# Four hundred places later in the scheduler's priorities for one stream of a two-stream kernel

## The chip, the cores and the metric

The kernel runs on one core of a Trainium2 chip. The core has a matrix engine (TensorE, PE in the profile, with a separate row PEld for its weight loads), a vector engine (VectorE, DVE), a scalar engine for activations (ScalarE, ACT), a general engine (GpSimd, POOL, hardly used here) and a queue that issues transfers (SyncE, SP). Each works through its own list of instructions in order; they wait for one another by semaphores. The metric is the device time of one execution in microseconds (us). Before the change the median of three runs is 2886.37 us (2886.14 to 2888.42).

## The reference

The reference runs two networks one after the other on 256 tokens of width 1024, in float32. The first block has four layers; each is a mixer, a gated projection and a layer norm:

```python
for i in range(DEPTH):                       # mixers: conv, ssm, rwkv7, conv
    y = mixer[i % 3](x, ...)
    r = DN_ALPHA * x + y
    r = r + (p[i] @ ple_proj[i]) * jax.nn.sigmoid(r @ ple_gate[i])
    x = layer_norm(r, ln_g[i], ln_b[i])
```

The second block has two layers over the tokens x and over a context ctx of another 256 rows of the same width. Each layer is a half feed-forward, a mixer in which the tokens also look at the context, and another half feed-forward:

```python
x   = half_ffn(x,   ..., ffn_w1[l, 0], ffn_w3[l, 0], ffn_w2[l, 0])
ctx = half_ffn(ctx, ..., ffn_w1[l, 0], ffn_w3[l, 0], ffn_w2[l, 0])
# half_ffn: h + 0.5 * gate * (silu(m @ w1) * (m @ w3)) @ w2, m = modulate(rms_norm(h))
```

The context does not depend on the first block. Its first feed-forward can therefore be computed while the first block's tokens are still on their way.

## The kernel before

Activations lie transposed: 8 chunks of 128 features by 256 tokens. A weight tile is 128 x 1024 floats: it is loaded into `w` (4 buffers), ACT rounds it to fp32r (`whi`, L601), DVE forms the rest (`wlo`, L602), with 4 buffers for each of the two. Activations are split in the same way into a hi and a lo part. A product of one output tile (128 features x 256 tokens) is 24 matmuls: for each of 8 chunks the three products hi x whi, lo x whi and hi x wlo (`mm3` and `mm3g`, L433 in the profile, where the engine's helper issues them). They accumulate in one of three PSUM buffers `ps_mm`. Smaller products use `ps_st`, `ps_ca` and `ps_cb`.

The program is written as generators. The stream X is the first block: `first()` runs conv, ssm, rwkv and conv, each followed by `ple_norm`. The stream C is the context: in the first block only `ffn(0, 0, ctx, 1)` runs of it, and as much of the next work as its `wait` allows. It has 44 tiles of the inner product (names `h1_hi`, `h1_lo`, `td`) and 24 of the outer (names `d1_hi`, `d1_lo`), 1584 matmuls. `Net.weave` takes turns: it steps the first stream that its own clock model holds for ready, X before C. The order in which steps are taken is the order of the program. A scheduler then sets the order on every engine: it takes what is ready by its own estimates, and among that what stands first in the priorities. An instruction's priority is its place in the program, kept in `tc.cur_priority`.

Names that the change and the text use: in `ple_norm` the sums `total` and `r` go to PE, then the squares `sq`, then `tc` (the reciprocal root on ACT and DVE), then `r` and `x` per chunk. In `rwkv` the shift `dx` and the blend `ta` follow on DVE, with `mix_hi` on ACT and `mix_lo` on DVE. The heads are small products in `ps_cb` and `ps_st` with copies `rw_a`, `rw_b` and `sv` between them. `gs` and `g` are the gated outputs of rwkv and conv before their output product. `xs` is a layer norm's result, split for the next product. The profile leaves out the numbers of names, so the context's `h1_hi` and `d1_hi` read `h_hi` and `d_hi` there.

Of the kernel before, what the change touches and what calls it, by code (L numbers as in the profile page):

```python
# [72 lines left out]
class Cols:  # L73
    def __init__(self):
        self.at, self.parts, self.n = {}, [], 0
# [190 lines left out]
class Stream:  # L266
# [2 lines left out]

    def __init__(self, net, gen, cache=None, shared=()):  # L270
        self.net, self.gen, self.cache, self.shared = net, gen, cache, shared
        self.ready, self.done, self.req = 0.0, False, None
        self.other, self.alone = None, set()
        self.advance(None)

# [164 lines left out]
class Net:  # L440
# [95 lines left out]
    def weave(self, streams, until=None):  # L536

        while not (until() if until else all(s.done for s in streams)):
            while self.side is not None and not self.hold and self.next <= self.now() and (self.V.t < self.now() + SLACK or self.next < self.now() - LATE):
                gap = next(self.side, None)  # L540
                if gap is None:
                    self.side = None
                else:
                    self.next = max(self.next, self.now() - LATE) + gap
            live = [s for s in streams if not s.done and not s.blocked()]
            s = next((s for s in live if s.ready <= self.now()), None)
            if s is None:
                s = next((s for s in streams if not s.done and s.blocked() and s.ready <= self.now()), None)
            if s is None:
                self.idle += min(s.ready for s in streams if not s.done) - self.now() + 1e-6  # L550
            else:
                s.step()

    def par(self, gens, width, last=None, most=3):


        todo, live = iter(gens), []
        last = [last, 0.0, None] if last else None
        while True:
            while len(live) < width and (not live or self.chains < most):  # L560
                g = next(todo, None)
                if g is None:
                    break
                live.append([g, 0.0, None])
                self.chains += 1
            both = live + ([last] if last else [])
            if not both:
                return
            c = next((c for c in both if c[1] <= self.now()), None)
            if c is None:  # L570
                yield Until(max(min(c[1] for c in both), self.now() + 0.01))
                continue
            self.end = self.now()
            try:
                y = c[0].send(c[2])
            except StopIteration:
                if c is last:
                    last = None
                else:
                    live.remove(c)  # L580
                    self.chains -= 1
                continue
            c[2] = None
            if isinstance(y, tuple):
                c[2] = yield y
            else:
                c[1] = y if isinstance(y, Until) else self.end
# [1319 lines left out]
def program(tc, ap, out, pat, cat):  # L1907
    nc = tc.nc
    with ExitStack() as es:
        n = Net(tc, ap, pat, cat, es)  # L1910
        X = Stream(n, n.first())
        X.step()
        nc.sync.dma_start(out=n.pr, in_=ap["params"])

        g = pat["gains"]
        nc.vector.tensor_scalar(out=n.pr[:, g:], in0=n.pr[:, g:], scalar1=-0.5, scalar2=None, op0=ALU.mult)
        nc.vector.tensor_scalar(out=n.p("b_kvn", 0, 2), in0=n.p("b_kvn", 0, 2), scalar1=4.0, scalar2=None, op0=ALU.mult)
        n.consts("base")
        c = n.big("cond0")

        def load_context():
            nc.sync.dma_start(out=n.ctx, in_=ap["ctxT"])
            yield 1.0

        n.side = itertools.chain(n.ssm_prep(), load_context(), n.ada(c, [(0, i, (1,), GAPS[0] / 2) for i in range(PARTS)]))
        n.weave([X], lambda: n.parts[0][1] > 1 and n.stage != "")

        def tokens():
            yield from n.ffn(0, 0, x, 0)
            yield from n.mixer_ab(ab, 0, x, 0)  # L1930
            yield from n.ffn(0, 1, x, 0)
            yield from n.ffn(1, 0, x, 0)
            yield from n.mixer_cd(1, x)
            yield from n.ffn(1, 1, x, 0, True)

        def context():
            yield from n.ffn(0, 0, n.ctx, 1)
            yield from n.wait("tokens")
            yield from n.mixer_ab(ab, 0, n.ctx, 1)
            order.reverse()  # L1940
            yield from n.ffn(0, 1, n.ctx, 1)
            yield from n.ffn(1, 0, n.ctx, 1)
            yield from n.cd_ctx(1)

        cache, shared = {}, ("cd_f", "cd_v", "cd_k") + tuple(f"ffn_{p}10" for p in ("in", "out0", "out1", "out2"))
        C = Stream(n, context(), cache, shared)
        n.weave([X, C], lambda: X.done)
        x = n.out_x
        n.consts("second", n.big("second"))
        ab = n.ab_shared()  # L1950
        n.came.add("tokens")
        X = Stream(n, tokens(), cache, shared)
        C.other, X.other = X, C
        order = [C, X]
        n.weave(order)
        nc.sync.dma_start(out=out, in_=x)
# [16 lines left out]
```

## Time and profile before

| | before |
|---|---|
| median of 3 runs | 2886.37 us |
| profiled execution | 2890.76 us |
| its span | 2889.0 us |
| granted clock, mean | 0.977 |
| DVE busy | 2134.0 us (74%) |
| ACT busy | 1606.4 us (56%) |

The profile is of one execution, and its times are measured against that execution's 2890.76 us, of which 2889.0 us are the span from the first instruction to the last. Busy is the union of an engine's instructions. Matmuls are pipelined: each lasts longer than the step from its start to the next one's. So steps are read from starts, and waits from the brackets at a row's end, which give the idle time ahead of a row and the engine and tile that ended it.

### The profile page before, as it was taken

The numbers are of one execution on the slowest core, as the hardware profiler recorded it, in microseconds if no ns is written. First come the engines' busy times: TensorE is split into PE (matmuls) and PEld (weight loads), VectorE is DVE, ScalarE is ACT, GpSimd is POOL, SyncE is SP. The second block draws the span as 40 slices with busy tenths as digits, with TensorE's granted clock in tenths as the row PEclk, the third lists the DMA queues.
The fourth block names the chain that finished last, engine by engine and source line by source line (L and its number), as shares of the span: only waits on it lengthen the run. The fifth ranks groups of instructions, "written<-read, shape, count | busy, mean of one in ns | idle before, by whom it ended". The sixth has DMA issues, their size and how long they took to land.

```text
span 2889.0 us, 58552 instructions
## 1 busy us (share of the span) xinstructions
PE 2749.4 (95%) x23798; PEld 2604.6 (90%) x23798; DVE 2134.0 (74%) x3953; ACT 1606.4 (56%) x2976; POOL 14.8 (1%) x41
## 2 busy tenths in 40 slices
PE   8978799899999998999999999999999999999999
PEld 8967799778998998998999978999999999996999
DVE  8877777666688788899789887777855556676655
ACT  5455555766555465877666766445422234466443
POOL 0000000000000000000000000000000000000000
PEclk9989799999999999999999999999999999999999
DMA  7743355201586665666576644666543433222554
GB/s 270 238 165 110 108 167 175 82 17 40 163 269 226 220 197 167 209 215 203 182 226 195 199 130 155 203 225 194 180 142 125 139 117 103 89 82 65 161 182 139
DMA packets 132751, 467.53 MB, mean 162 GB/s; under 512 B 14720, under 2 KB 19072, under 8 KB 131840
## 3 DMA queue, kind: packets, MB, share of 16 engines
q1 hardware_dynamic: 132480, 463.78, 50.0%
q8 instruction: 187, 3.06, 0.4%
q14 instruction: 84, 0.69, 0.1%
HBM read 462.67 MB, written 1.05 MB: 161 GB/s over the span
## 4 chain that ended last, share of the span: by engine, by line
PE 72%; DVE 12%; DMA 7%; ACT 6%; issue 3%; SPq 0%; ACTq 0%; DVEq 0%
PE ps_mm L433 62%; PE ps_ca L433 5%; DMA w<-in_ada_dram 5%; DVE wlo L602 3%; PE ps_cb L433 2%; DVE junk L1379 2%; PE ps_st L433 2%; DVE ssm_m L403 2%; ACT whi L601 2%; DVE tc L403 1%; PE ps_cb L437 1%; ACT rw_b L403 1%; ACT L403 1%; ACT tc L403 1%; DMA w<-in_ab_in_dram 1%
## 5 line engine op out<-in xcount | busy, mean ns | idle before, releaser
L601 ACT ACTIVATE whi<-w 128x1024 fp32r<-128x1024 f32 (+1 forms) x687 | 715.9, 1043 | 740.2 <-PE ps_mm L433 488.1
L602 DVE TENSOR_TENSOR wlo<-w,whi 128x1024 fp32r<-128x1024 f32 (+1 forms) x687 | 825.6, 1203 | 239.2 <-ACT whi L601 236.8
L433 PE MATMUL ps_mm<-h_hi,whi 128*128 128x256 f32 x3024 | 873.1, 290 | 17.1 <-ACT h_hi L403 12.4
L433 PE MATMUL ps_mm<-h_hi,wlo 128*128 128x256 f32 x3024 | 859.5, 285 | 9.5 <-DVE wlo L602 9.5
L433 PE MATMUL ps_mm<-h_lo,whi 128*128 128x256 f32 x3024 | 856.5, 284 | 0.6 <-DVE h_lo L403 0.5
L433 PEld LDWEIGHTS ps_mm<-h_hi,whi 128*128 128x128 f32 x3024 | 573.6, 190 | 25.8 <-ACT h_hi L403 15.1
L433 PEld LDWEIGHTS ps_mm<-h_hi,wlo 128*128 128x128 f32 x3024 | 573.3, 190 | 12.2 <-DVE wlo L602 11.5
L433 PEld LDWEIGHTS ps_mm<-h_lo,whi 128*128 128x128 f32 x3024 | 577.5, 191 | 5.2 <-DVE h_lo L403 1.9
L1379 DVE SCALAR_TENSOR_TENSOR junk<-w,cond 128x1024 bf16<-128x1024 f32 x288 | 351.7, 1221 | 145.0 <-DMA w<-in_ada_dram 144.1
L433 PE MATMUL ps_mm<-d_hi,whi 128*128 128x256 f32 x1232 | 355.7, 289 | 4.1 <-DVE ctx L403 3.0
L433 PE MATMUL ps_mm<-d_hi,wlo 128*128 128x256 f32 x1232 | 350.4, 285 | 1.5 <-DVE wlo L602 1.5
L433 PE MATMUL ps_mm<-d_lo,whi 128*128 128x256 f32 x1232 | 349.2, 283 | 0.4 <-DVE d_lo L403 0.4
L433 PEld LDWEIGHTS ps_mm<-d_hi,whi 128*128 128x128 f32 x1232 | 232.3, 189 | 8.7 <-issue 5.7
L433 PEld LDWEIGHTS ps_mm<-d_lo,whi 128*128 128x128 f32 x1232 | 234.0, 190 | 3.4 <-issue 1.2
L433 PEld LDWEIGHTS ps_mm<-d_hi,wlo 128*128 128x128 f32 x1232 | 232.1, 189 | 2.8 <-DVE wlo L602 2.0
L403 DVE TENSOR_TENSOR td<-td,ps_mm 128x256 f32<-128x256 f32 x154 | 64.4, 418 | 70.0 <-PE ps_mm L433 68.9
L403 ACT ACTIVATE d_hi<-td 128x256 fp32r<-128x256 f32 x154 | 63.0, 409 | 89.5 <-DVE td L403 88.7
L403 ACT ACT_TABLE_LOAD x78 | 100.1, 1283 | 2.1 <-PEq L1964 0.7
L433 PE MATMUL ps_mm<-x_hi,whi 128*128 128x256 f32 x256 | 73.5, 287 | 12.0 <-ACT whi L601 12.0
L403 ACT ACTIVATE tc<-tc 128x256 f32<-128x256 f32 x182 | 75.1, 413 | 5.6 <-DVE tc L403 2.6
L433 PE MATMUL ps_mm<-xs_hi,whi 128*128 128x256 f32 x256 | 73.4, 288 | 4.8 <-ACT xs_hi L403 4.4
L403 ACT ACTIVATE td<-ps_mm 128x256 f32<-128x256 f32 x154 | 57.4, 374 | 32.9 <-PE ps_mm L433 32.3
(467 smaller groups left out, 5270.5 us busy)
## 6 DMA issues: line engine op xcount, KB each, us to landing
w<-in_ffn_in_dram SPq DMA_DIRECT2D x268, 512.0 KB, 4.2
w<-in_ada_dram SPq DMA_DIRECT2D x168, 512.0 KB, 4.3
w<-in_ffn_out_dram SPq DMA_DIRECT2D x96, 512.0 KB, 4.1
w<-in_conv_in_dram SPq DMA_DIRECT2D x64, 512.0 KB, 4.7
w<-in_ffn_out_dram SPq DMA_DIRECT2D x48, 384.0 KB, 3.1
w<-in_ab_in_dram SPq DMA_DIRECT2D x34, 512.0 KB, 4.4
w<-in_ple_gate_dram SPq DMA_DIRECT2D x32, 512.0 KB, 4.5
w<-in_conv_out_dram SPq DMA_DIRECT2D x16, 512.0 KB, 5.2
```

Of the source, the lines that this page charges most:

```text
L403: return f(**kw)
L433: self.t.matmul(out, lhsT=lhsT, rhs=rhs, start=start, stop=stop)
L437: self.t.transpose(out, in_, ident)
L601: nc.scalar.activation(out=hi[:, :n], in_=w[:, :n], func=AF.Copy)
L602: nc.vector.tensor_tensor(out=lo[:, :n], in0=w[:, :n], in1=hi[:, :n].bitcast(F32), op=ALU.subtract)
L1379: nc.vector.scalar_tensor_tensor(out=self.junk, in0=w, scalar=1.0, in1=cb[:, s], op0=ALU.mult, op1=ALU.mult, accum_out=m[:, t, s:s + 1])
```

## The change

A stream gets a number `later`, which is 0 unless set. While `weave` steps a stream, it raises the priority counter by that number and lowers it again afterwards. For the context's stream it is 400 as long as the first block's tokens run, and 0 after that. So every instruction that a step of the context issues there (transfers, splits, matmuls, ACT and DVE operations) counts as standing 400 instructions later than it is written. The steps are taken in the same order as before.

```diff
-        self.ready, self.done, self.req = 0.0, False, None
+        self.ready, self.done, self.req, self.later = 0.0, False, None, 0
...
             else:
+                self.tc.cur_priority += s.later
                 s.step()
+                self.tc.cur_priority -= s.later
...
         C = Stream(n, context(), cache, shared)
+        C.later = 400
         n.weave([X, C], lambda: X.done)
+        C.later = 0
```

The instructions on every engine are the same; only their order differs, from the second layer's end to the first steps of the second block. Three places follow.

On DVE, in the mixing ahead of rwkv's first product, where `wlo_4642` and `wlo_4675` belong to the context, `wlo_4711` to the tokens' first product, and `mix_lo_4524` and `mix_lo_4742` are the first and the second blend. Before:

```order
L403 SCALAR_TENSOR_TENSOR ta_4563<-dx_4522,pr_58,x_4383 128x256
L403 TENSOR_SCALAR dx_4522<-x_4383 128x1
L602 TENSOR_TENSOR wlo_4608<-w_4606,whi_4607 128x1024
L403 TENSOR_TENSOR mix_lo_4524<-ta_4563,mix_hi_4523 128x256
L403 SCALAR_TENSOR_TENSOR ta_4569<-dx_4522,pr_58,x_4383 128x256
L602 TENSOR_TENSOR wlo_4642<-w_4640,whi_4641 128x1024
L403 TENSOR_TENSOR mix_lo_4524<-ta_4569,mix_hi_4523 128x256
L602 TENSOR_TENSOR wlo_4675<-w_4673,whi_4674 128x1024
L602 TENSOR_TENSOR wlo_4711<-w_4709,whi_4710 128x1024
```

With the change:

```order
L403 TENSOR_TENSOR mix_lo_4742<-ta_4923,mix_hi_4741 128x256
L403 TENSOR_TENSOR mix_lo_4742<-ta_4959,mix_hi_4741 128x256
L403 SCALAR_TENSOR_TENSOR ta_4995<-dx_4522,pr_58,x_4383 128x256
L403 SCALAR_TENSOR_TENSOR ta_5033<-dx_4522,pr_58,x_4383 128x256
L403 SCALAR_TENSOR_TENSOR ta_5069<-dx_4522,pr_58,x_4383 128x256
L403 TENSOR_TENSOR mix_lo_4742<-ta_4995,mix_hi_4741 128x256
L403 TENSOR_TENSOR td_4604<-td_4604,ps_mm_4612 128x256
L403 SCALAR_TENSOR_TENSOR ta_5105<-dx_4522,pr_58,x_4383 128x256
L604 TENSOR_TENSOR wlo_4642<-w_4640,whi_4641 128x1024
L403 TENSOR_TENSOR d1_lo_3163<-td_4604,d1_hi_3162 128x256
L604 TENSOR_TENSOR wlo_4675<-w_4673,whi_4674 128x1024
L604 TENSOR_TENSOR wlo_4711<-w_4709,whi_4710 128x1024
```

The context's `wlo_4642` and the two behind it stood among the last operations of the first blend; now they stand behind the second blend as well and behind three operations of a third.

On PE, in one of the last heads of rwkv, between two steps of the tokens (`ps_cb_8709` and `ps_cb_8734`). Before:

```order
L433 MATMUL ps_cb_8709<-rw_a1_5704 64x64
L433 MATMUL ps_mm_8721<-h1_hi_3095,wlo_8717 128x256
L433 MATMUL ps_mm_8721<-h1_hi_3095,whi_8716 128x256
L433 MATMUL ps_mm_8721<-h1_lo_3096,whi_8716 128x256
L433 MATMUL ps_mm_8721<-h1_hi_3095,wlo_8717 128x256
L433 MATMUL ps_mm_8721<-h1_hi_3095,whi_8716 128x256
L433 MATMUL ps_mm_8721<-h1_lo_3096,whi_8716 128x256
L433 MATMUL ps_mm_8721<-h1_hi_3095,wlo_8717 128x256
L433 MATMUL ps_mm_8721<-h1_hi_3095,whi_8716 128x256
L433 MATMUL ps_mm_8721<-h1_lo_3096,whi_8716 128x256
L433 MATMUL ps_mm_8721<-h1_hi_3095,wlo_8717 128x256
L433 MATMUL ps_cb_8734<-rw_a1_5704,rw_b1_5705 64x64 x2
```

With the change, from the same step to the two after the next:

```order
L433 MATMUL ps_cb_8709<-rw_a1_5704 64x64
L433 MATMUL ps_mm_8363<-d1_hi_3162,whi_8358 128x256
L433 MATMUL ps_mm_8363<-d1_lo_3163,whi_8358 128x256
L433 MATMUL ps_mm_8363<-d1_hi_3162,wlo_8359 128x256
L433 MATMUL ps_cb_8734<-rw_a1_5704,rw_b1_5705 64x64 x2
L433 MATMUL ps_mm_8363<-d1_hi_3162,whi_8358 128x256
L433 MATMUL ps_mm_8363<-d1_lo_3163,whi_8358 128x256
L433 MATMUL ps_mm_8363<-d1_hi_3162,wlo_8359 128x256
L433 MATMUL ps_cb_8753<-sv0_4504,rw_b1_5705 64x64 x2
L433 MATMUL ps_cb_8758<-rw_b1_5705,sv0_4504 64x64
```

Ten context matmuls (tile 8721) stood between the two steps; now three of an earlier tile (8363) stand there, and three ahead of the step that follows.

On PE, between rwkv's last gate product (`ps_mm_9419`) and its output product (`ps_mm_9495`). Before, with 21 more of tile 9458 behind:

```order
L433 MATMUL ps_mm_9419<-mix_lo_8972,whi_9414 128x256
L433 MATMUL ps_mm_9419<-mix_hi_8971,wlo_9415 128x256
L433 MATMUL ps_mm_9458<-h1_hi_3095,whi_9453 128x256
L433 MATMUL ps_mm_9458<-h1_lo_3096,whi_9453 128x256
L433 MATMUL ps_mm_9458<-h1_hi_3095,wlo_9454 128x256
```

With the change:

```order
L433 MATMUL ps_mm_9419<-mix_hi_8971,whi_9414 128x256
L433 MATMUL ps_mm_9419<-mix_lo_8972,whi_9414 128x256
L433 MATMUL ps_mm_9419<-mix_hi_8971,wlo_9415 128x256
L433 MATMUL ps_mm_9458<-h1_hi_3095,whi_9453 128x256
L433 MATMUL ps_mm_9495<-gs_hi_9150,whi_9490 128x256
L433 MATMUL ps_mm_9495<-gs_lo_9151,whi_9490 128x256
L433 MATMUL ps_mm_9495<-gs_hi_9150,wlo_9491 128x256
L433 MATMUL ps_mm_9495<-gs_hi_9150,whi_9490 128x256
```

Before, all 24 matmuls of the context's tile 9458 stood between the two; now the first of them does, and the other 23 stand among later steps of the tokens.

## Rows read from the trace of the kernel before

**Rows 1.** The page, span and busy time of each engine

```profile
span 2889.0 us, 58552 instructions
...
PE 2749.4 (95%) x23798; PEld 2604.6 (90%) x23798; DVE 2134.0 (74%) x3953; ACT 1606.4 (56%) x2976; POOL 14.8 (1%) x41
```

**Rows 2.** Stretches: length, busy by engine (PE, PEld, DVE, ACT, POOL), PEclk, DMA share, GB/s

```profile
409.00:451.00 42.00, 37.25 (x282) 36.41 (x281) 37.66 (x88) 28.80 (x55) 0.00 (x0) 0.92 0.41 137
529.00:772.00 243.00, 226.17 (x3533) 191.55 (x3528) 153.05 (x370) 154.06 (x419) 0.00 (x0) 0.98 0.17 52
566.00:580.00 14.00, 11.73 (x306) 10.85 (x302) 3.61 (x7) 6.81 (x19) 0.00 (x0) 1.00 0.01 2
884.00:893.00 9.00, 8.31 (x52) 8.20 (x53) 8.23 (x18) 6.37 (x17) 0.00 (x0) 0.72 0.46 140
```

**Rows 3.** Timeline of PE ahead of the mixing: start, duration, what, [idle before]

```profile
436.28 0.39 PE L433 MATMUL ps_mm<-h_hi,whi 128*128 128x256 f32 x1 [1.13 <-ACT td L403]
...
440.40 0.58 PE L433 MATMUL ps_mm<-h_hi,wlo 128*128 128x256 f32 x1 [3.62 <-DVE wlo L602]
440.78 0.42 PE L433 MATMUL ps_mm<-h_hi,whi 128*128 128x256 f32 x1
441.00 0.41 PE L433 MATMUL ps_mm<-h_lo,whi 128*128 128x256 f32 x1
```

**Rows 4.** Timeline of DVE, the layer norm's end and the mixing

```profile
427.01 3.25 DVE L403 SCALAR_TENSOR_TENSOR r<-r,pr,tc 128x256 f32<-128x256 f32 x8
430.18 0.42 DVE L403 TENSOR_TENSOR d_lo<-td,d_hi 128x256 fp32r<-128x256 f32 x1
430.52 0.42 DVE L403 TENSOR_TENSOR dx<-x 128x255 f32<-128x255 f32 x1
430.85 0.15 DVE L403 TENSOR_SCALAR dx<-x 128x1 f32<-128x1 f32 x1
430.92 0.42 DVE L403 TENSOR_TENSOR dx<-x 128x255 f32<-128x255 f32 x1
431.25 0.48 DVE L403 SCALAR_TENSOR_TENSOR ta<-dx,pr,x 128x256 f32<-128x256 f32 x1
431.64 0.15 DVE L403 TENSOR_SCALAR dx<-x 128x1 f32<-128x1 f32 x1
...
432.83 0.42 DVE L403 TENSOR_TENSOR td<-td,ps_mm 128x256 f32<-128x256 f32 x1
433.16 0.76 DVE L403 TENSOR_TENSOR mix_lo<-ta,mix_hi 128x256 fp32r<-128x256 f32 x2
433.83 0.48 DVE L403 SCALAR_TENSOR_TENSOR ta<-dx,pr,x 128x256 f32<-128x256 f32 x1
...
439.13 1.22 DVE L602 TENSOR_TENSOR wlo<-w,whi 128x1024 fp32r<-128x1024 f32 x1
```

**Rows 5.** Timeline of ACT in the same layer norm

```profile
425.95 1.06 ACT L601 ACTIVATE whi<-w 128x1024 fp32r<-128x1024 f32 x1
```

**Rows 6.** Timeline of all engines around one step of the last heads

```profile
758.25 0.29 PE L433 MATMUL ps_cb<-rw_a 128*64 128x64 f32 x4
...
758.66 0.22 ACT L403 ACTIVATE rw_a<-ps_cb 128x64 f32<-128x64 f32 x1 [1.32 <-PE ps_cb L433]
...
760.10 0.33 PE L433 MATMUL ps_cb<-rw_a,rw_b 64*64 64x64 f32 x4
```

**Rows 7.** Timeline of PE and of DVE ahead of rwkv's output product

```profile
807.29 0.28 PE L433 MATMUL ps_mm<-h_hi,whi 128*128 128x256 f32 x1
...
810.17 0.28 PE L433 MATMUL ps_mm<-gs_hi,whi 128*128 128x256 f32 x1
...
812.25 0.42 DVE L403 TENSOR_TENSOR gs_lo<-ta,gs_hi 128x256 fp32r<-128x256 f32 x1
```

**Rows 8.** Timeline of PE and of DVE ahead of the second conv's output product

```profile
979.61 0.29 PE L433 MATMUL ps_mm<-d_hi,whi 128*128 128x256 f32 x1
...
982.49 0.29 PE L433 MATMUL ps_mm<-g_hi,whi 128*128 128x256 f32 x1
...
983.95 0.42 DVE L403 TENSOR_TENSOR g_lo<-ta,g_hi 128x256 fp32r<-128x256 f32 x1
```

**Rows 9.** Timeline of PE, the second conv's first matmul

```profile
884.69 0.58 PE L433 MATMUL ps_mm<-xs_hi,whi 128*128 128x256 f32 x1 [4.45 <-ACT xs_hi L403]
```

## The prediction

> **What bounds the kernel now.** I read the page's head first: TensorE (PE) is busy 2749.4 of 2889.0 us, 95% [rows 1]. So the time is the matmuls plus PE's waits, and a change that only reorders can move nothing but the waits and the clock. I then asked for busy time by stretch [rows 2]. From 409 to 451 us (the first block's second layer norm, then the token mixing of RWKV) PE is busy 37.25 of 42 us. In the heads of RWKV, 529 to 772 us, it is idle 16.8 us of 243, and most of that lies early, before there is any context work to fill with: 566 to 580 us alone has 2.27 us idle in 14. The third layer norm (884 to 893 us) ran at a granted clock of 0.72. Everywhere else in the stretch that the change touches (314 to about 1166 us) PE hardly waits, because the context's feed-forward matmuls stand in its queue between the steps of the tokens' serial chains. These are the cover that the change moves. The third view is the timeline of single stretches, for what each wait ends on [rows 3 to 9].
>
> **What the change removes, adds and moves.** It adds and removes no operation: the same matmuls, weight splits and transfers run, and the weights' transfers keep their order but for a few places. What moves is the order on PE, DVE and ACT between 314 and about 1166 us. Two effects follow. The tokens' small operations on ACT and DVE get ahead of the context's: ACT's and DVE's part of the token chains can end earlier. Against this, the context's matmuls no longer stand in blocks between token steps, and the splits of the context's weights (whi on ACT, wlo on DVE) stand later. But the weights still come in program order through four buffers, and PE's own queue still has context matmuls ahead of token matmuls that need later weights. So a late wlo of the context can stop everything.
>
> *The layer norm before the mixing (409 to 451 us).* This is the largest term. Before, PE waits twice, 1.13 us and 3.62 us [rows 3], the second for a wlo that DVE began at 439.13, between two mix operations [rows 4]. The matmul that uses the next wlo (wlo_4642) comes 24 matmuls later. In rows 3 these come 0.21 us apart, so it starts near 440.40 + 24 x 0.21 = 445.4. With the change wlo_4642 stands on DVE behind the first two mixes whole and three operations of a third, as the order shows. Ahead of it, counted in that order after the eight r: 8 dx at 0.33, 8 single columns with the next step at 0.07, 19 ta at 0.39, 16 mix_lo at 0.33, two td at 0.33 and one d_lo at 0.34, each from the starts in rows 4, or 2.6 + 0.6 + 7.4 + 5.3 + 0.7 + 0.3 = 16.9 us. The r began at 427.01 and took 3.25; ahead of them ACT now has one more split (1.06, rows 5) between Ln and Exp, which puts them about 1 us later, so DVE has done them near 431.2. wlo_4642 then starts at 448.1 at the earliest and ends near 449.4; x on ACT is put off too (a split, a table load, d_hi and a td now stand ahead of it), so I take 450. PE arrives near 438 and waits some 12 us instead of 4.75. At the same matmul it is 450 - 445.4 = 4.6 us late if the matmuls after it go at the full clock, and up to 2.2 us more if again 24 of them go at 0.21 instead of 0.12. I take +6; the bounds are +3 (DVE does the mixes in parts while ACT is behind, or later waits of before vanish) and +10 (x a further 3 us late).
>
> The clock in that stretch: after the wait of 3.62 us the matmuls start 0.21 us apart [rows 3], twice the 0.12 that 24 matmuls in 2.88 us show [rows 7], so PE was granted the lower of its two levels. The Trainium skill says in "TensorE: Matmul & The Clock Gate", section "HAM oscillation", that waits of PE for data throttle it again and that each such wait pays for its slow start anew; the trace agrees here. By that rule the long wait costs the 2.2 us in full (+6.8 instead of my +6).
>
> *The heads of RWKV.* Here a step on PE is followed by a copy on ACT and the next step. In [rows 6] the step at 758.25 ends at 758.54, its copy runs 758.66 to 758.88, and the next step could follow near 759.0; PE fills with twelve context matmuls (1.44 us) and takes the step up at 760.10. Before, 47 runs of context matmuls stand in the heads, 504 matmuls with the 96 that end them, hardly any run under ten where it covers a step. With the change most runs are one to four matmuls (0.12 to 0.48 us), about 240 in all, and 253 stand together after the last head. A fill of 0.36 us against a step's latency of 0.45 leaves 0.1 us; where the step has a copy twice as long, 0.3. From the other side: without fill, from 566 to 580 us, PE is 16% idle [rows 2]. The heads from 577 to 772 us without the 408 context matmuls are 195 - 49 = 146 us, of which 16% is 24 us to be covered. Before, 49 us of context covered it wherever it fell; now 29 us do, in pieces cut to the scheduler's estimates. If every piece fits, the cost is 0; if half of the 24 us stays open, 12. I take a fifth, +5.
>
> *The output of RWKV.* Before, 24 context matmuls run from 807.29 to 810.17, and then the 192 with gs begin [rows 7]. The last gs_lo starts on DVE at 812.25 and is there at 812.67, when the eighth of k (0.36 us each) is due at 810.17 + 7 x 0.36 = 812.69: no wait. With the change one context matmul stands there and gs begins 23 x 0.12 = 2.8 us earlier, but its last gs_lo cannot come earlier, as it hangs on matmuls of the tokens and now stands behind a wlo. The context's 23 matmuls come after, spread over PE's next steps, where they give back up to half a microsecond: +2.3 (bounds 0.5 and 3.5).
>
> *The output of the second conv.* The same: 24 context matmuls stand from 979.61 and the g begin at 982.49; the last g_lo ends at 983.95 + 0.42 = 984.37 [rows 8] and is due at 982.49 + 7 x 0.36 + 0.12 = 985.13. The slack is 0.76, the move 2.76: +2.0 (bounds 0 and 2.5).
>
> *The rest*: at the first output of the block, the third layer norm, the fourth and the hand-over to the second block, the same matmuls stand in nearly the same order, with small moves both ways. I count them at 0 (bounds -4 and +4); the cover there is the context's own runs of 46 to 300 matmuls, which are left whole.
>
> Sum: 6 + 5 + 2.3 + 2.0 = +15.3 us on the profiled execution's 2890.8 us, or 2906.1. That execution lies 4.4 above the median of the runs, so against 2886.4 it is 2901.7.
>
> **Rivals.**
> *No change.* PE does the same matmuls, and a wait cut out at one place comes back at another: the context matmuls that no longer cover a step are still there to cover the next one. For it: the runs before the outputs are only put off by some hundred matmuls, and the heads' pieces might fit. Against it: the wait for wlo_4642 is covered by nothing. With LN at +3 and the heads at 0 the outputs at +1 remain: +4, so 2890.
>
> *Faster.* The mechanism is the third layer norm: xs, which the second conv's matmuls wait for, come sooner since d_hi, td and d_lo of the context no longer stand ahead of the tokens on ACT and DVE. Its price is the wait of 4.45 us [rows 9] and the low clock around it (0.72 over 9 us is 5 us at half speed, 2.5 lost): -7, so 2879. It decides if the wait in the mixing stays at its 4.75 us and the heads' pieces fit; against it, in the order of that layer norm only a few context operations stand ahead of xs even before.
>
> *Slower by more.* After the long wait, or in the heads, where PE now has many short gaps, the clock falls to its lower level for longer: 20 us at half speed cost 10, so 2912. Against it: 566 to 580 us is 16% idle at a clock of 1.00 [rows 2].
>
> **How the numbers follow.** My forecast has 0.60 (2893 to 2910), no change 0.17, faster 0.10, the low clock 0.13. What can be told from no change here is 0.2%, 5.8 us: faster means under 2880.6, slower over 2892.1. That gives 0.10 faster, 0.18 the same, 0.72 slower. The range that leaves out two in ten goes from 2884 (half of the cases faster or little changed) to 2914.
>
> **What would show it.** Right: a PE wait of 9 us or more near 440 us for wlo, with DVE busy on dx, ta and mix_lo through it; in the heads more PE idle (20 to 29 us instead of 16.8) and a long run of context matmuls after them; gs and g waiting 2 to 3 us on gs_lo and g_lo. Wrong: a wait near 440 us no longer than 5 us (DVE was not the one), heads with no more idle time than before, or a shorter wait for xs near 885 us that pays for the rest.

## The result, and the profile after

The change makes the kernel slower: 2907.61 us median of four runs (2903.28 to 2912.19) against 2887.39 us before on the same chip, a ratio of 1.0062 (95% interval 1.0045 to 1.0079), some 18 us. Run again (e1) the ratio was 1.0067 (1.0054 to 1.008). The forecast was 2901.7 in a range of 2884 to 2914, and slower with 0.72. The profiled execution after took 2911.79 us.

The head of the page shows the same work in a longer span: of the 21 us that the span grows, 8 are PE's busy time [rows 1], for the same 23798 matmuls, and 13 are idle time of PE. DVE's busy time is the same.

```profile
span 2910.0 us, 58561 instructions
...
PE 2757.6 (95%) x23798; PEld 2609.4 (90%) x23798; DVE 2133.1 (73%) x3953; ACT 1605.8 (55%) x2976; POOL 14.8 (1%) x41
```

To see where the time went, I laid the two traces on one another by work done: for a moment of before, I looked up when the kernel compared had done matmuls of the same total, each kind of matmul counted at its median step in the trace of before. The difference is that kernel's delay at that moment, in us. Where the order differs and has not caught up, the figure is off by a microsecond or two. The row e11 is a yardstick: as shown below, that kernel has the order of before on every engine, so its row is what one execution differs from another by.

| at (us of before) | 313 | 409 | 465 | 772 | 792 | 815 | 893 | 990 | 1170 | 1300 | 2800 |
|---|---|---|---|---|---|---|---|---|---|---|---|
| after | 0.9 | -1.2 | 7.5 | 9.1 | 13.4 | 16.2 | 17.9 | 19.8 | 14.3 | 15.0 | 21.0 |
| e1, the same again | 0.3 | -1.6 | 7.2 | 8.9 | 12.8 | 16.0 | 17.5 | 21.2 | 16.0 | 15.2 | 14.2 |
| e11, the order of before | -1.0 | -1.0 | -1.1 | -1.2 | -1.3 | -1.3 | 1.7 | 2.6 | 1.4 | 1.7 | 5.7 |

Five things are to be read off: a gain of 2 us up to 409; a loss of 8.7 us in the layer norm ahead of the mixing (409 to 465); 1.6 in the heads (to 772); 4.3 between the heads and the z product (to 792), and 2.8 ahead of rwkv's output (to 815). Up to 815 us e11 moves by 0.3 us, so these five stand clear of it. Behind that some microseconds come and go, in e11 too (3.0 lost from 815 to 893), and what the first profile lost in the second block (1300 to 2800, +6.0) the second did not lose (-1.0), so that is one execution's and not the order's.

The largest piece, as the timeline of PE after shows it (the stretch of [rows 3]: start, duration, what, idle before and its releaser):

```profile
440.23 0.55 PE L433 MATMUL ps_mm<-h_hi,whi 128*128 128x256 f32 x1 [3.37 <-DVE td L403]
440.58 0.42 PE L433 MATMUL ps_mm<-h_lo,whi 128*128 128x256 f32 x1
...
448.61 0.55 PE L433 MATMUL ps_mm<-mix_hi,whi 128*128 128x256 f32 x1 [7.61 <-DVE td L403]
...
450.05 0.58 PE L433 MATMUL ps_mm<-h_hi,wlo 128*128 128x256 f32 x1 [0.67 <-DVE wlo L604]
```

PE idles 11.65 us in three waits, where it idled 4.75 before. Two of the three, 10.98 us, end on td, DVE's reading of a finished context tile, which frees one of the three `ps_mm` buffers. The timeline of DVE says when the two td were ([rows 4] is its stretch before):

```profile
428.55 3.26 DVE L403 SCALAR_TENSOR_TENSOR r<-r,pr,tc 128x256 f32<-128x256 f32 x8
431.73 0.42 DVE L403 TENSOR_TENSOR dx<-x 128x255 f32<-128x255 f32 x1
...
439.68 0.41 DVE L403 TENSOR_TENSOR td<-td,ps_mm 128x256 f32<-128x256 f32 x1
...
447.71 0.42 DVE L403 TENSOR_TENSOR mix_lo<-ta,mix_hi 128x256 fp32r<-128x256 f32 x1
448.05 0.41 DVE L403 TENSOR_TENSOR td<-td,ps_mm 128x256 f32<-128x256 f32 x1
448.38 0.48 DVE L403 SCALAR_TENSOR_TENSOR ta<-dx,pr,x 128x256 f32<-128x256 f32 x1
448.77 1.22 DVE L604 TENSOR_TENSOR wlo<-w,whi 128x1024 fp32r<-128x1024 f32 x1
```

DVE works from 431.73 to 448.05 without a pause, on the blends but for one td at 439.68 and one d_lo; only then come the second td and, 0.7 us later, wlo_4642. The granted clock in 409 to 462 us fell to 0.84, as the view by stretch shows (columns as in [rows 2]). First the same stretch of before, at 0.94, then two of after:

```profile
409.00:462.00 53.00, 48.25 (x374) 47.41 (x373) 47.94 (x106) 35.54 (x67) 0.00 (x0) 0.94 0.46 150
```

```profile
409.00:462.00 53.00, 41.32 (x303) 40.11 (x303) 42.83 (x98) 30.48 (x62) 0.00 (x0) 0.84 0.36 115
538.00:781.00 243.00, 227.05 (x3501) 191.49 (x3498) 150.77 (x366) 151.31 (x416) 0.00 (x0) 0.98 0.15 49
```

The last row is the stretch of the heads, 243 us long as in [rows 2]: PE is idle 15.95 us in it, against 16.8 before. Two more waits, from the timeline of PE, stand where before had none, ahead of the z product and of rwkv's output (the stretch of [rows 7]):

```profile
794.00 0.80 PE L433 MATMUL ps_mm<-mix_hi,whi 128*128 128x256 f32 x2 [2.28 <-ACT mix_hi L403]
...
824.60 0.39 PE L433 MATMUL ps_mm<-gs_lo,whi 128*128 128x256 f32 x1 [1.29 <-DVE gs_lo L403]
...
826.52 0.38 PE L433 MATMUL ps_mm<-gs_hi,whi 128*128 128x256 f32 x1 [0.82 <-ACT gs_hi L403]
```

At the second conv's output ([rows 8]) it waits 1.41 and 0.42 us, and the wait for xs of [rows 9] is still 4.27:

```profile
902.89 0.66 PE L433 MATMUL ps_mm<-xs_hi,whi 128*128 128x256 f32 x2 [4.27 <-ACT xs_hi L403]
...
998.85 0.39 PE L433 MATMUL ps_mm<-g_hi,whi 128*128 128x256 f32 x1 [1.41 <-ACT te L403]
...
1002.17 0.38 PE L433 MATMUL ps_mm<-g_lo,whi 128*128 128x256 f32 x1 [0.42 <-DVE g_lo L403]
```

### The profile page after: what moved, and what is told of

The parts are those of the page before. It is cut to its first block, busy times and chain, and to the rows that moved or that the text cites. A ratio compares the mean times of both kernels' runs of the same rounds, so it can differ in the third digit from the quotient of the medians.

```text
span 2910.0 us, 58561 instructions
## 1 busy us (share of the span) xinstructions
PE 2757.6 (95%) x23798; PEld 2609.4 (90%) x23798; DVE 2133.1 (73%) x3953; ACT 1605.8 (55%) x2976; POOL 14.8 (1%) x41
## 4 chain that ended last, share of the span: by engine, by line
PE 70%; DVE 13%; DMA 8%; ACT 6%; issue 3%; SPq 0%; DVEq 0%; ACTq 0%
PE ps_mm L433 60%; DMA w<-in_ada_dram 6%; PE ps_ca L433 5%; DVE wlo L604 4%; PE ps_cb L433 2%; DVE junk L1381 2%; DVE ssm_m L403 2%; ACT whi L603 2%; PE ps_st L433 2%; DVE tc L403 1%; PE ps_cb L437 1%; ACT rw_b L403 1%; ACT tc L403 1%; ACT L403 1%; DVE ta L403 1%
## 5 line engine op out<-in xcount | busy, mean ns | idle before, releaser
L433 PE MATMUL ps_mm<-h_hi,whi 128*128 128x256 f32 x3024 | 870.1, 289 | 19.8 <-ACT h_hi L403 12.8
```

What stands on the lines that cost most here:

```text
L433: self.t.matmul(out, lhsT=lhsT, rhs=rhs, start=start, stop=stop)
```

## The experiments

Delays at equal work, as above, of the experiments' profiles:

| at (us of before) | 313 | 409 | 465 | 772 | 792 | 815 | 893 | 990 | 1170 | 2800 |
|---|---|---|---|---|---|---|---|---|---|---|
| e2, off in the norm | 1.4 | -0.4 | -1.1 | 0.4 | 2.5 | 5.6 | 8.4 | 11.2 | 5.5 | 5.2 |
| e3, on only in the norm | 0.6 | 0.6 | 8.6 | 9.5 | 9.8 | 10.2 | 13.3 | 13.0 | 7.6 | 4.1 |
| e4, weights old | 1.4 | -0.8 | 8.7 | 11.5 | 13.8 | 16.8 | 17.6 | 20.7 | 20.1 | 18.1 |
| e5, readers old | 2.0 | 2.6 | 11.1 | 13.1 | 17.1 | 21.3 | 23.2 | 25.8 | 19.8 | 23.0 |
| e6, matmuls later | 0.3 | 0.8 | 1.9 | 5.9 | 8.4 | 12.3 | 13.5 | 15.9 | 12.6 | 10.9 |
| e7, heads only | -1.0 | -1.0 | -1.0 | 0.8 | 8.8 | 9.9 | 12.9 | 13.5 | 12.6 | 16.1 |
| e8, z only | 1.3 | 1.3 | 1.3 | 1.1 | 3.0 | 5.3 | 5.5 | 6.3 | 4.6 | 4.6 |
| e9, splits first | 3.4 | 3.5 | -1.9 | 0.4 | 0.4 | 0.4 | -0.1 | 0.1 | -3.5 | -3.1 |
| e10, context earlier | -0.5 | -0.4 | 1.6 | 53.5 | 54.6 | 58.3 | 64.2 | 65.9 | 61.3 | 64.6 |
| e11, the order of before | -1.0 | -1.0 | -1.1 | -1.2 | -1.3 | -1.3 | 1.7 | 2.6 | 1.4 | 5.7 |
| e12, all splits first | -1.7 | -4.1 | -11.0 | -9.8 | -9.7 | -5.7 | -5.7 | -3.8 | -15.1 | -8.5 |

**Does it come from places, and do they add up?** The flag `zone` is set by the first block as it goes on.

```diff
-                self.tc.cur_priority += s.later
+                later = s.later if self.zone in ZONES else 0
+                self.tc.cur_priority += later
                 s.step()
-                self.tc.cur_priority -= s.later
+                self.tc.cur_priority -= later
```

e1, ZONES is everything:

> The change as it stands, once more, with a flag that is on in every stretch of the first block, so that single stretches can be left out in the runs beside it. Its first four times were 2903.3, 2903.4, 2911.8 and 2912.2 us. Both theories: 2903 to 2912 us, about 16 to 25 us over the kernel before. A second profile shows which of the differences from before belong to the order (they come again) and which to the one execution: the wait near 440 us (11 us in parts) and the 2.3 us at 794 us should come again; the 6.5 us that the first profile lost after 1220 us, where the order is the same as before, need not.

Measured: 2909.83 us against 2891.44, 1.0067 (1.0054 to 1.008). The waits came again to a tenth (7.6, 3.4 and 0.7 us near 440 us), and the loss in the second block did not.

e2, all but the norm ahead of RWKV and the first blend:

> The 400 is on everywhere but in the layer norm ahead of RWKV and in its first blend (until RWKV's first product). Theory 'places' (each place where the context's operations now stand behind the tokens' has its own price, and the prices add up): the wait near 440 us is again about 5 us, and the time falls by the 8.4 us that the comparison of the two profiles shows there, to 12 us over before, 2895 to 2903 us. Rival 'one late chain' (what is late at one place is late because of the first, so that without it the rest goes too): within 4 us of before, 2886 to 2891 us.

Measured: 2896.12 us, 1.002 (1.0011 to 1.0028). The waits near 440 us are 3.6 and 1.1 us, as before.

e3, only there:

> The 400 is on only in the layer norm ahead of RWKV and in its first blend. 'Places': 8 us over before, 2892 to 2898 us, with the waits near 440 us as in the changed kernel, and no lag that grows after 470 us. 'One late chain': most of the 20 us, 2901 us or more.

Measured: 2898.99 us, 1.0025 (1.0014 to 1.0035), 1 us above what "places" gave. At 772 us e2 is 0.4 us late, e3 9.5, and e1, with both, 8.9. So up to there the places add up, and "one late chain" falls. Past 815 us this is less clean: e3, whose order is that of before there, loses 3 us by 893, as e11 does, and wins 5.4 from 990 to 1170. Over the whole run the two together (0.2 and 0.25%) give 0.45 of the 0.67%; whether the other 6 us are real is not settled. By their intervals the two give 0.25 to 0.63% together and the change 0.54 to 0.80%, and at the hand-over (990 to 1170 us) the profiles of e3, e7, e8 and e11, whose order on PE there is that of before, win 0.9 to 5.4 us.

**What does PE wait for in the norm?** A context tile needs its weights split (whi, wlo) and a free `ps_mm` buffer, and the buffer is freed by td. Both stand later on DVE. e4 leaves the first at its old place, e5 the second, e6 both:

```diff
# e4: in Stream.step, within a weave that adds s.later
+            self.net.tc.cur_priority -= self.later
             w = self.net.get(self.req)
+            self.net.tc.cur_priority += self.later
# e6: weave adds nothing; in TensorE.matmul
+        net.tc.cur_priority += net.later
         self.t.matmul(out, lhsT=lhsT, rhs=rhs, start=start, stop=stop)
+        net.tc.cur_priority -= net.later
# e5: as e6, and the same two lines around net.get
```

> The context's loads and weight splits (w, whi, wlo) keep their old place, all its other instructions stand 400 later. So wlo_4642 stands ahead of the second blend again, while td_4465 and td_4604, whose reading sets free a PSUM buffer, stand still later. Theory 'late splits' (the prediction's: PE waits for wlo): the wait near 440 us is 5 us or less again and the time falls by some 8 us, to 2895 to 2903 us. Rival 'PSUM' (the profile puts 3.4 and 7.6 us of the wait on td, which is late on DVE for the same reason): the wait stays 8 us or more, ended by td, and the time is within 4 us of the changed kernel's.

Measured: 2911.75 us, 1.0072 (1.006 to 1.0084). The waits add up to 10.5 us, against 11.65. First the timeline of PE, then that of DVE:

```profile
439.29 0.58 PE L435 MATMUL ps_mm<-h_hi,whi 128*128 128x256 f32 x1 [2.20 <-ACT td L405]
...
441.40 0.58 PE L435 MATMUL ps_mm<-h_hi,wlo 128*128 128x256 f32 x1 [1.32 <-DVE wlo L606]
...
453.39 0.58 PE L435 MATMUL ps_mm<-h_hi,whi 128*128 128x256 f32 x1 [7.02 <-DVE td L405]
```

```profile
440.13 1.21 DVE L606 TENSOR_TENSOR wlo<-w,whi 128x1024 fp32r<-128x1024 f32 x1
...
442.00 1.22 DVE L606 TENSOR_TENSOR wlo<-w,whi 128x1024 fp32r<-128x1024 f32 x1
443.13 0.42 DVE L405 TENSOR_TENSOR mix_lo<-ta,mix_hi 128x256 fp32r<-128x256 f32 x1
443.47 1.22 DVE L606 TENSOR_TENSOR wlo<-w,whi 128x1024 fp32r<-128x1024 f32 x1
...
452.93 0.41 DVE L405 TENSOR_TENSOR td<-td,ps_mm 128x256 f32<-128x256 f32 x1
```

The three wlo shown are there by 445 us, and PE stands until the td of 452.93 has read its tile. "Late splits" alone, the prediction's reason, falls. This td is 4.9 us later than in the changed kernel, since five weight splits stand among the blends ahead of it here.

> The mirror of e4: loads, weight splits and matmuls of the context stand 400 later, its ACT and DVE operations on results (td, d_hi, d_lo) keep their old place. On DVE td_4465 and td_4604 stand early again, wlo_4642 behind the second blend. If only the PSUM buffer counted, the wait near 440 us falls to 5 us or less. Theory 'either': whichever of the two stands late on DVE ends the wait, since both stand behind the same 16 us of blends: 9 us or more again, now ended by wlo. Time under 'either' 2904 to 2914 us, else some 8 us less.

Measured: 2910.62 us, 1.0082 (1.0066 to 1.0097). Now td comes early, and the long wait ends on wlo, as PE's timeline shows (the wait of 3.78 us on mix_hi comes again in e6, 3.79):

```profile
444.87 0.55 PE L437 MATMUL ps_mm<-mix_hi,whi 128*128 128x256 f32 x1 [3.78 <-ACT mix_hi L405]
...
454.35 0.58 PE L437 MATMUL ps_mm<-h_hi,wlo 128*128 128x256 f32 x1 [8.72 <-DVE wlo L610]
```

> Only the context's matmuls stand 400 later; its loads, splits and operations on results keep their old place. Theory 'either': the wait near 440 us is 6 us or less, as before, and the matmul order (single fills in the heads, outputs of rwkv and conv that start at once) costs what it did: some 10 us over before, 2896 to 2904 us. If the place of the matmuls on PE were the cause of that wait, it would stay 9 us or more and the time at 2904 us or more.

Measured: 2901.83 us, 1.0044 (1.003 to 1.0058). Here is PE's timeline of the same stretch:

```profile
443.04 0.55 PE L435 MATMUL ps_mm<-mix_hi,whi 128*128 128x256 f32 x1 [3.79 <-ACT mix_hi L403]
...
445.49 0.58 PE L435 MATMUL ps_mm<-h_hi,wlo 128*128 128x256 f32 x1 [1.68 <-DVE wlo L608]
```

5.5 us of waits, and 1.1 us lost from 409 to 465. So "either" holds: the td and the wlo both stand behind the blends, and each of them alone, left late, makes a wait of 7 to 9 us. The other 10 us of e6 are the price of the matmuls' order on PE: 4.0 in the heads, 2.5 at z, 3.9 ahead of rwkv's output.

**The heads and the z product.** ZONES is one stretch each:

> The 400 is on only from RWKV's first product to its last head. The prediction gave the heads +5 us (0 to 12); the two profiles compared show +1.6 there. 'Places': the heads lose 0 to 3 us by their end (about 782 us), and what the order leaves of context work for the products behind them decides the rest: 2888 to 2896 us. If the prediction's size was right and hidden in the changed kernel by the late start: +5 us or more at 782 us.

Measured: 2900.42 us, 1.0045 (1.0028 to 1.0061); the time is above what was expected. The heads lose 1.8 us up to 772, as in the changed kernel (1.6). But then 8.0 us go by 792. At 782 us, the place that the expectation names, the loss is already 5.6: there PE is in the context's matmuls that the heads put off, and it waits 2.12 us among them and 2.25 ahead of the z product. ACT's timeline shows what stands in the way, a split whose weights, those of the z product, are not there yet:

```profile
778.07 1.06 ACT L604 ACTIVATE whi<-w 128x1024 fp32r<-128x1024 f32 x1 [3.69 <-DMA w<-in_rwkv_z_dram]
779.73 1.06 ACT L604 ACTIVATE whi<-w 128x1024 fp32r<-128x1024 f32 x1 [0.60 <-DMA w<-in_rwkv_z_dram]
780.69 0.37 ACT L403 ACTIVATE td<-ps_mm 128x256 f32<-128x256 f32 x1
```

Behind it on ACT stand the td that frees PE's buffer and the last head's reciprocal root, with whose result DVE ends the head; ACT's mix_hi for the z product waits for that. The changed kernel has this wait as well, 1.99 us, ahead of the root's last step, as ACT's timeline shows:

```profile
787.04 1.06 ACT L603 ACTIVATE whi<-w 128x1024 fp32r<-128x1024 f32 x1 [1.99 <-DMA w<-in_rwkv_z_dram]
```

> The 400 is on only from the last head to the end of the product with the z weights. The two profiles compared show +4.3 us between 782 and 792 us, a term that the prediction lacked: PE waits 2.3 us for mix_hi, because a weight split that waits for its transfer stands on ACT ahead of the last head's reciprocal root, and then runs at the low clock for 3.4 us. 'Places': the wait at that place comes again (2 us or more) and the lag at 792 us is 2.5 to 5 us. Rival: it needs the backlog of context work that the heads leave (253 matmuls in one run); then no wait there and a time as before, 2886 to 2892 us.

Measured: 2893.8 us, 1.0016 (1.0004 to 1.0028). Waits of 0.53 and 0.82 us come in place of the 2.3, and 1.9 us of delay. So the loss at z is mostly the heads' backlog, which neither theory had as it is: the stretch that shows the wait is not the one whose order makes it. ACT's wait for the z weights ahead of that product says the same: e1, e2 and e4 to e7, which all leave the backlog, have it (0.9 to 3.7 us the longest), before, e3 and e8 do not. Here the places do not add up: e7 and e8 alone lose 8.0 and 1.9 us from 772 to 792, and both together, in the changed kernel, 4.3.

**Turned round.** e9 gives the context's weights alone 400 places earlier (`weave` adds nothing):

```diff
+            self.net.tc.cur_priority -= self.later
             w = self.net.get(self.req)
+            self.net.tc.cur_priority += self.later
```

> The turn of the change for the weights alone: the context's loads and splits (w, whi, wlo) stand 400 earlier than written while the first block runs, all its other instructions where they stood before. wlo_4608 and wlo_4642 then stand on DVE ahead of the first blend. If a context matmul waits for whatever of its needs stands behind the tokens' work on DVE, the wait of 3.6 us for wlo near 440 us goes, and with it part of the low clock: 3 to 6 us less than before, 2881 to 2885 us. Rival: the splits (1.1 us on ACT, 1.2 on DVE each) put the tokens' chain off by as much as they save: within 3 us of before.

Measured: 2889.6 us against 2892.45, 0.9991 (0.9982 to 1.0). The time is what the rival gave, within 3 us of before. But no wait over 1 us is left near 440 us, and 5.4 us are won from 409 to 465; 3.4 us of delay that its profile had at 313 us, where its order on PE and DVE is that of before, and 2.3 lost in the heads hide most of it there.

e10 gives the change the other sign:

```diff
-        C.later = 400
+        C.later = -100
```

> The change with the other sign: all of the context's instructions stand 100 earlier while the first block runs. The matmuls ahead of rwkv's and conv's outputs stay whole, the splits and td come earlier on DVE, the tokens' small operations later. 'Places': the wait near 440 us is 3 us or less, but the tokens' chains in the layer norms end 1 to 2 us later each: 2882 to 2890 us. If what counts is only that the tokens go first, it is slower than before by as much as the change was: 2900 us or more.

Measured: 2950.05 us, 1.0195 (1.0169 to 1.0221). I had expected it faster, and it is slower by more than the rival gave, too. The norm is as expected (2.0 us lost, no wait over 0.8), but in the heads it loses 52 us, most of it from 700 to 800. The view by stretch shows this:

```profile
700.00:740.00 40.00, 38.42 (x497) 30.62 (x497) 24.48 (x69) 18.58 (x54) 0.00 (x0) 0.96 0.16 58
740.00:752.00 12.00, 12.00 (x118) 9.00 (x117) 3.15 (x6) 4.51 (x14) 0.00 (x0) 0.98 0.14 45
752.00:788.00 36.00, 36.00 (x176) 25.69 (x174) 5.62 (x11) 8.05 (x19) 0.00 (x0) 0.50 0.09 30
```

PE counts as busy, with 118 matmuls in 12 us and 176 in 36, the latter at a clock of 0.50, the lower of the two levels. PE's timeline says what they are:

```profile
747.13 0.38 PE L433 MATMUL ps_mm<-d_hi,wlo 128*128 128x256 f32 x1
747.44 0.33 PE L433 MATMUL ps_cb<-rw_b 128*64 128x64 f32 x2
747.70 0.39 PE L433 MATMUL ps_mm<-d_hi,whi 128*128 128x256 f32 x1
748.02 0.33 PE L433 MATMUL ps_cb<-rw_b 128*64 128x64 f32 x2
```

With the context first, the scheduler puts its matmuls one by one between the small steps of the heads: from 700 to 788 us about 50 stand alone, in all the heads of before 6. From the start of a single one to the small pair behind it go 0.31 and 0.32 us, and 0.26 from there to the next, where large matmuls in a row start 0.12 us apart. So neither sign is right for the heads. Blocks as before cost less than either; a version that puts whole blocks off was not run.

e11 was to be on only in the stretch up to the norm, where the change is ahead by 2 us. ZONES is `a` alone:

> The 400 is on only until the layer norm ahead of RWKV, where the comparison of the two profiles shows the change ahead by 2 to 2.6 us (at 357 us). 'Places': it is ahead by 2 us at 409 us too, and keeps it or loses it to waits in the norm that do not depend on PE: 2884 to 2889 us, not slower than before. Rival: what is put off there is missing as cover later: 2890 us or more.

Measured: 2890.36 us, 1.0 (0.9989 to 1.0011). This run did not test what it was for. `a` ends when the first conv's first product begins; the first layer norm and the mixer behind it run under `n0`, which e1 and e2 have and e11 does not. Its trace has every operation of PE, DVE and ACT in the order of before, so it is the kernel before once more. The other runs settle the question. From 313 to 409 us the four profiles in which the context's td, d_hi and d_lo stand later win 1.8 to 2.2 us (after, e1, e2, e4), the four with the order of before win nothing (e3, e7, e8, e11: 0.0), and e5 and e6, where those keep their old place, lose 0.5 to 0.6. So the 2 us are the order's, and come from td, d_hi and d_lo standing later.

**A version that beats both.** e12 puts every weight split of the program 100 places earlier, and nothing else:

```diff
+        self.tc.cur_priority -= 100
         nc.scalar.activation(out=hi[:, :n], in_=w[:, :n], func=AF.Copy)
         nc.vector.tensor_tensor(out=lo[:, :n], in0=w[:, :n], in1=hi[:, :n].bitcast(F32), op=ALU.subtract)
+        self.tc.cur_priority += 100
```

> Every weight split of the program (whi on ACT, wlo on DVE, of tokens and context, in both blocks) stands 100 earlier in the priorities; nothing else moves in them. If late splits are what PE waits for in the rest of the program too (the page has 14.0 us of waits on whi and 11.5 on wlo), some go: 3 to 12 us less than before, 2877 to 2886 us. Rival: the splits stand ahead of the tokens' small operations, and those chains are what most of the other waits end on: 2890 us or more.

Measured: 2882.3 us against 2892.45, 0.9962 (0.9948 to 0.9976): about 11 us faster than before (0.38% of 2892), and faster than the changed kernel by both ratios. That PE waited for late splits shows: its waits on wlo fall from 11.5 to 2.4 us in all, those on whi from 14.0 to 10.3. The norm is the surest place, with 6.9 us won from 409 to 465 and the clock at 1.00 all through, in the view by stretch. 4.0 are lost ahead of rwkv's output (792 to 815), the hand-over gives 11.3 from 990 to 1170, part of which kernels with the order of before win there as well, and 6.6 are lost again by 2800:

```profile
405.00:455.00 50.00, 49.72 (x406) 49.07 (x405) 45.54 (x99) 37.64 (x68) 0.00 (x0) 1.00 0.52 169
```

## Why the prediction was right, point by point

The sign, the size and the main place came as forecast: +15.3 us predicted, 18 to 20 measured, inside the range. The sum came closer than its terms: the norm cost 2.7 us more than its term and the heads 3.4 less, and the sum lacks 4.3 us lost at z and 2 won ahead of the norm. That these nearly cancel is luck. The rivals "no change" and "faster" fell; the wait for xs, on which "faster" rested, is 4.27 us instead of 4.45.

*The signs set down for right and wrong*: the long run of context matmuls behind the heads came (253, from 761.0 to 791.4 us), and so did the 2 us of gs, 1.29 and 0.82. DVE was busy through the wait near 440 us, but no single wait was 9 us and the long ones were not for wlo. And one sign of being wrong came too: the heads have no more idle time than before.

*The layer norm*: predicted +6 (3 to 10), measured +8.7 to 8.8 by the profiles and +8.0 where it alone is changed (e3, 409 to 465). The count of DVE's work was close: r began at 428.55 where I had 428.0, and wlo_4642 started at 448.77 where I had 448.1 at the earliest. What I lacked is the second chain. I named wlo as what PE waits for, and 10.98 of the 11.65 us ended on td and a `ps_mm` buffer; e4 shows that with wlo in time the wait is nearly as long. That I named wlo alone did not show in the size, because both stand behind the same blends: at the matmul that needs wlo_4642 (450.05 us) the changed kernel is 4.5 us late at equal work, where I had 4.6. That is luck. The clock's share was under-sized: the matmuls behind that one start 0.21 us apart until 455.8 and add some 3 us, where I took 1.4 and had 2.2 as the most. The rest of the 8.7 is the lead of 1.2 us that the kernel had at 409 us and lost here.

*The heads*: predicted +5 (0 to 12), measured +1.6 to 1.8. The term was mis-sized: the pieces fit the steps better than I allowed, as the idle time of 15.95 us says. The cover of before was in smaller pieces than I had read, too: 20 of its 46 runs in the heads have fewer than ten matmuls. But putting the work off was not free. It came due at the next chain, the blend for z, with 4.3 us (8.0 in e7), a place that the prediction does not have. Together the two are close to the +5, by accident.

*rwkv's output*: predicted +2.3, measured +2.8, with a wait of 1.29 us on gs_lo, which it names, and one of 0.82 on gs_hi.

*The second conv's output*: predicted +2.0. There are waits (1.41 and 0.42, only the second on g_lo), and the delay grows by 1.9 us up to 990, but about as much is given back by 1012. In sum I can't tell it from nothing.

*The rest*, predicted 0 within 4: a gain of 2 us ahead of the norm, which is the order's; 1.5 to 1.7 lost by the third layer norm, where e11 loses 3.0 with the order of before; 5.2 to 5.5 won at the hand-over, where profiles with the order of before win up to 5.4. The 6 us in the second block are one execution's.

*Slower by more, by the clock*: in time the result lies about midway between the forecast and this rival's 2912. But it did not come as priced: the heads ran at 0.98 as before, and in the norm the matmuls at the lower clock add the 3 us above, not 10.

## What to carry to other kernels

When a priority is put off, list for each engine what the put-off instructions hold (weight buffers, PSUM buffers) and who needs that: an instruction off the critical path that frees a buffer is on it as soon as the buffers run out. Weight splits were worth going first even where their stream is the less urgent one (e12); that the reads that free PSUM gain by going first was not run alone, only what it costs when they go late (e4). Filler cut into short runs or single matmuls cost time whichever way it was moved (e6, e10). Compare traces by work done and not by time: the place that shows a wait need not be the place whose order makes it.

## What the runs showed of the hardware that was not expected

PE's change between matmuls of different kind costs more than either: 0.26 to 0.32 us from start to start when one matmul of 128x256 and two small ones alternate, against 0.12 in a row of the large ones (e10). It is not the clock of e10: in the heads of before, at 0.98, the small step behind a single large matmul starts 0.31 us after it (6 times), and behind a run of them 0.21 us after the last (39 times). Whether shape, type or something else of the two kinds makes it, no run shows. The profile calls PE busy all through, and the granted clock still went to 0.50 for 36 us (752 to 788 us of e10), in a stretch without any idle time on PE's rows, whose ends are modelled. So busy time by itself says neither that PE is fast nor that its clock will hold.
